# A macaron decoder layer in split float32: the first feature pair by plain products, no splits on GpSimd, and 20 weights' lower parts made ahead

## The chip, the cores and the metric

The kernel runs on one core of a Trainium2 chip. The metric is the device time of one execution in microseconds; a profiled execution gives a span (first to last instruction) and a trace. In the trace PE is the matrix engine (TensorE) and PEld its weight loads, DVE is VectorE, ACT is ScalarE, POOL is GpSimd, SP is the engine whose queue issues the kernel's DMAs.

## The reference

One layer on x of 512 tokens by 1024, all in float32:

```python
x = x + 0.5 * rms_norm(swiglu_1(rms_norm(x)))
x = x + rms_norm(hybrid_mixer(rms_norm(x)))
x = x + 0.5 * rms_norm(swiglu_2(rms_norm(x)))

def swiglu(h, w_gate, w_up, w_down):          # 1024 -> 2816 -> 1024
    return (silu(h @ w_gate) * (h @ w_up)) @ w_down
```

The mixer projects h with w_in (1024 x 2840) to the queries, keys and values of two head groups: 4 differential-attention heads, and 8 heads of sparse attention with a compressed branch (31 windows of keys and values through a small MLP, cmp_k_w1 and cmp_v_w1, 2048 x 256 each), a selected branch and a window branch. Their outputs go together through w_out.

## The kernel before, in words

**Split operands.** A float32 operand is split into a high part (a copy rounded to the matrix engine's fp32r) and a lower part (the rest), and each product is made as three: high x high, high x low, low x high. The high part is a cast on ACT (or DVE), the lower part a subtraction. `split` makes both; with `sbuf=True`, which is for sources in SBUF, the lower part may run on DVE or on POOL.

**Feed-forward.** Gate and up weights are handled in 11 pairs c of two 128-feature tiles. For a pair, the 2x2 block product (two halves of the 1024 inputs, two feature tiles, two halves of the tokens) is made with seven products in place of eight, a Winograd form of Strassen's method. It needs sums of weight blocks (`quad`, L501), sums of token blocks (`combos`, L466) and sums of the results (`tail`, L620). One product is 24 matmuls of 256 columns for gate and up together (`product`, L592). `SEQ` lists products in order; the first 12 entries weave pair 0 and pair 1. `prenorm` normalises and transposes the tokens in four blocks t; blocks 0 and 1 give the operands of products 1 and 2, and all others need blocks 2 and 3 too. The raw weights of even pairs stand in four "raw" buffers, those of odd pairs in "M" (pair 1 in "A"). The hidden tiles of the first three pairs are kept in DRAM for a while. Then `down_mm` multiplies 22 pieces of w_down (L675).

**Pieces.** `piece` loads 512 KB of a weight into a raw buffer and splits it into the ring (12 buffers, six pieces). w_down, w_in, cmp_*_w1 and w_out all come this way: pieces wp0 to 21 of the first feed-forward, 22 to 29 of w_in for keys, values and gates, 30 to 37 of the compression, 38 to 53 of w_in for the queries and the differential heads, 54 to 61 of w_out, then the second feed-forward.

**Order.** Nothing is issued in program order. `Graph.order` is a list scheduler: each operation has a cost per engine that may do it, a level (longest way to the end) plus a bias from the table `BIAS`, keyed by engine and kind of operation, and the tiles that it needs from pools of limited room (`ROOM`, `CAPS`). An operation marked `port` isn't put on DVE while one is on POOL, and the other way round, in the planner's own clock. What comes out is a fixed order for each engine's queue.

Of the kernel before, what the change touches and what calls it, by code (L numbers as in the profile page):

```python
# [40 lines left out]
WARM = (10, 0, 4)  # L41
# [18 lines left out]
    "ACT:xat>xa": 293.6, "ACT:xat>xa@ACT": 202.7, "ACT:xat>xa@DVE": 2.6, "ACT:xct>xc": 130.8, "ACT:xct>xc@ACT": 3.5,  # L60
    "ACT:xct>xc@DVE": -75.7, "ACT:xi>n_ss": 151.7, "ACT:xj>n_ss": -17, "ACT:xm>n_ss": 71.9, "ACT:xrk>Xk": 27.7,
    "ACT:xrk>Xk@ACT": 215.9, "ACT:xrk>Xk@DVE": 88.2, "ACT:xrv>Xv": 21.1, "ACT:xrv>Xv@DVE": 185.7, "ACT:z>o_ss": -397,
    "DVE:acc>oN": -22.3, "DVE:cd_t>kc": -2.6, "DVE:ck>kcT": 33, "DVE:cmask>cmb": -15, "DVE:cmask>gates": -21.9,
    "DVE:cmk>uk": -47.8, "DVE:cmv>uv": -143.2, "DVE:cv>vc": -114.3, "DVE:d>d_p": 5.9, "DVE:d_acc>o": -23.6,
    "DVE:d_r>d_p": 57.3, "DVE:d_t>d_th": -89.6, "DVE:dkt>dk": -5, "DVE:dl>d_r": 15.8, "DVE:dl>do_r": -95.2,
    "DVE:do_rr>o": 29.9, "DVE:do_t>oTd": -159.1, "DVE:fa>fh": -99.8, "DVE:fa>fhs": -11.9, "DVE:fb>fp_": -0.2,
    "DVE:fc>fp_": -0.1, "DVE:fc__sg>fh": -132.7, "DVE:fh>fhl@DVE": 14, "DVE:fh>fhl@POOL": 311.6, "DVE:fhr>fhl": 105.8,
# [10 lines left out]
    "DVE:rawff2q>fqv": -3, "DVE:rawff2q>fqw": 168, "DVE:wrv>wv": 105, "DVE:xaf0>xat": -287, "DVE:xaf1>xat": -136.2,
    "DVE:xag>xat": -23.4, "DVE:xat>xa": -88.7, "DVE:xat>xa@DVE": -123.4, "DVE:xat>xa@POOL": -416.3,
    "DVE:xat>xat": 117.5, "DVE:xcf0>xct": -36.7, "DVE:xcg>xct": 73.7, "DVE:xct>xc@DVE": -82.9, "DVE:xct>xct": -126.9,  # L80
    "DVE:xi>n_xn": 708.4, "DVE:xj>n_xn": -7.5, "DVE:xm>n_xn": 164.6, "DVE:xrk>Xk": 54.2, "DVE:xrk>Xk@DVE": -2.7,
    "DVE:xrk>Xk@POOL": -3.8, "DVE:xrv>Xv": -333.6, "DVE:xrv>Xv@POOL": 55.6, "DVE:z>o_yg": -29.8, "PE:cd>kc": 86.1,
    "PE:d_th>d_acc": 10, "PE:dkd>dk": 5.9, "PE:fqw>fa": 40.2, "PE:fqw>fb": 1946, "PE:fqw>fc": 144.3,
    "PE:gh>g_": 714.9, "PE:k__dup>kT": 107.9, "PE:n_p>n_th": 513.5, "PE:n_th>acc": 1025.2, "PE:n_xn>n_t": 678.6,
    "PE:n_xn>xa": 5.3, "PE:n_xn>xb": -7, "PE:n_xn>xc": 3.3, "PE:nc_h>acc": -114.8, "PE:nc_pc>nc_h": -56.2,
    "PE:o>oTd": 45.6, "PE:qTd>d_p": 32.9, "PE:qTn>n_p": -100.2, "PE:qTn>nc": -153.5, "PE:qdd>qTd": -46.3,
    "PE:qdn>qTn": 30.3, "PE:uk>hTk": 48.3, "PE:uv>hTv": 162.9, "PE:warm>warm": -220.7, "PE:wk>ck": 142.1,
    "PE:wp>cd": 2, "PE:wp>dkd": 3.2, "PE:wp>fc__": 5.5, "PE:wp>fy": 24.4, "PE:wp>pv": 4.5, "PE:wp>qdd": -27.8,
    "PE:wp>qdn": 241.5, "PE:wp>uk": 119.8, "PE:wp>uv": -58.6, "PE:wp>z": 7.7, "PE:wv>cv": -146.5, "POOL:Xk>Xk": -91.6,
    "POOL:Xv>Xv": -59.2, "POOL:do_r>do_rr": -5.4, "POOL:do_ss>do_r": -23.4, "POOL:n_ss>n_r": 32,  # L90
    "SP:cmask>cmask": 21.4, "SP:dmask>dmask": -101.9, "SP:fhd>fhr": -72.1, "SP:g_ff1_norm_post>g_ff1_norm_post": 29.3,
    "SP:g_ff2_norm_post>g_ff2_norm_post": -22.6, "SP:g_ff2_norm_pre>g_ff2_norm_pre": -6.7,
    "SP:g_mix_norm_post>g_mix_norm_post": 14, "SP:g_mix_norm_pre>g_mix_norm_pre": 215.9, "SP:gr>gr": 233.5,
    "SP:gsub>gsub": -81.4, "SP:pev>pev": 67.7, "SP:raw>raw": 272.8, "SP:rawff2q>rawff2q": 516.3,
    "SP:trig>trig": -45.2, "SP:wrk>wrk": 5.2, "SP:wrv>wrv": -22.2, "SP:x>xm": -63.6, "SP:x>xo": -51, "SP:xi>xi": 92.4,
    "SP:xj>x": 4.2, "SP:xj>xj": 60.7, "SP:xm>x": -19.8, "SP:xm>xm": -31, "SP:xo>xo": 30,
# [3 lines left out]
    "s_yg": 66, "s_h": 14, "s_v": 36, "s_p": 5, "s_t": 22, "s_o": 16, "s_oT": 15, "b_t": 22, "b_x": 20, "b_gu": 6, "s_ch": 8, "s_f": 10, "s_q": 8,  # L100
# [173 lines left out]
def layer(ctx: ExitStack, tc: tile.TileContext, io, out):  # L274
# [36 lines left out]
    def f32(ap):  # L311
        return ap.bitcast(F32)
# [17 lines left out]
    def piece(src, a, b, pool="ring"):  # L330
        i = len(wp)
        n = a * b
        raw, w = f"raw{i}", f"wp{i}"
        new(raw, "raw", [P, 1024])
        pdma.append(load(raw, lambda: T[raw][:, :n].rearrange("p (a b) -> p a b", a=a), src, chain="dma"))
        if pool == "ring":
            parts[i] = [f"wp{i}h", f"wp{i}l"]
            for k in parts[i]:
                new(k, pool, [P, 1024], F32R)
            hi, lo = (lambda k=k: T[k][:, :n] for k in parts[i])  # L340
        else:
# [24 lines left out]
    def split(src, hi, lo, n, r, kh, kl, chain=None, sbuf=False, after=()):  # L366
# [4 lines left out]
        def low():  # L371
            (V if o.done == "DVE" else nc.gpsimd).tensor_sub(lo(), src(), f32(hi()))  # L372
# [74 lines left out]
    def new_combos(name):  # L447
        for m in range(1, 8):
            new(f"{name}{m}", "A", [P, 2, 4, 256], F32R)

    def combos(xT, t, banks):

        u, fl = t % 2, (lambda k: (lambda: T[k].rearrange("p (k q) -> p k q", k=4)))
        cs = slice(u * P, (u + 1) * P)

# [909 lines left out]
```

## Time and profile before

| | |
|---|---|
| median of 3 runs | 1043.58 us (1043.29 to 1046.88) |
| profiled execution | 1042.48 us, span 1040.7 us |
| mean granted clock of the span | 0.990 |
| busy: PE, PEld, DVE, ACT, POOL | 97%, 88%, 75%, 53%, 10% |
| HBM read, written | 104.00 MB, 9.44 MB |

Busy time of PE is modelled from the starts of pipelined matmuls, so a PE that is busy all the time need not be at its peak. Idle time counts only on an engine that others wait for.

### The profile page before, as it was taken

The numbers are of one execution on the slowest core, as the hardware profiler recorded it, in microseconds if no ns is written. First come the engines' busy times: TensorE is split into PE (matmuls) and PEld (weight loads), VectorE is DVE, ScalarE is ACT, GpSimd is POOL, SyncE is SP. The second block draws the span as 40 slices with busy tenths as digits, with TensorE's granted clock in tenths as the row PEclk, the third lists the DMA queues.
The fourth block names the chain that finished last, engine by engine and source line by source line (L and its number), as shares of the span: only waits on it lengthen the run. The fifth ranks groups of instructions, "written<-read, shape, count | busy, mean of one in ns | idle before, by whom it ended". The sixth has DMA issues, their size and how long they took to land.

```text
span 1040.7 us, 17111 instructions
## 1 busy us (share of the span) xinstructions
PE 1005.4 (97%) x6540; PEld 913.2 (88%) x6540; DVE 783.5 (75%) x1528; ACT 548.5 (53%) x1128; POOL 104.3 (10%) x107
## 2 busy tenths in 40 slices
PE   7999999999999989899999999999999999999997
PEld 6999999999888869787888888889999999988886
DVE  6999998987332477977888799799999988743324
ACT  7554555556222254676877787485555555632302
POOL 2100000001000040131100153221000000000001
PEclk9999999999999999999999999999999999999999
DMA  7145433217432342611010236114434231473202
GB/s 243 59 145 149 147 109 123 70 53 250 175 102 81 88 143 82 223 43 60 23 40 22 60 107 238 41 42 162 139 125 146 73 108 41 143 262 101 81 21 81
DMA packets 78723, 114.53 MB, mean 110 GB/s; under 512 B 9905, under 2 KB 60337, under 8 KB 78642
## 3 DMA queue, kind: packets, MB, share of 16 engines
q1 hardware_dynamic: 78642, 113.45, 32.8%
q8 instruction: 51, 0.84, 0.3%
q14 instruction: 30, 0.25, 0.1%
HBM read 104.00 MB, written 9.44 MB: 109 GB/s over the span
## 4 chain that ended last, share of the span: by engine, by line
PE 79%; DVE 14%; issue 2%; ACT 2%; DMA 1%; POOL 1%; SPq 0%; DVEq 0%; POOLq 0%; ACTq 0%
PE ff2y L675 12%; PE ff1y L675 11%; PE ff1b L592 7%; PE ff2b L592 6%; PE ff1a L592 5%; PE ff1c L592 5%; PE ff2c L592 4%; PE ff2a L592 4%; PE z L1221 3%; PE n_t L1117 2%; PE n L1007 1%; PE acc L363 1%; PE n L1008 1%; PE acc L364 1%; DVE ff2p L620 1%
## 5 line engine op out<-in xcount | busy, mean ns | idle before, releaser
L1020 ACT ACTIVATE n_p<-n_p,n_nm 128x128 f32<-128x128 f32 (+3 forms) x64 | 35.3, 553 | 11.9 <-DVE n_nm L1018 11.5
L372 DVE TENSOR_TENSOR n_th<-n_t,n_th 128x512 fp32r<-128x512 f32 x40 | 26.0, 685 | 11.0 <-ACT n_th L369 11.0
L1018 DVE CUSTOM_DVE_ANT_0 n_p<-n,dmb 128x128 f32<-128x128 f32 (+3 forms) x64 | 28.3, 485 | 3.4 <-PE n L1008 1.6
L404 POOL TENSOR_SCALAR o_ms<-o_ss 128x1 f32<-128x1 f32 x12 | 4.5, 372 | 240.1 <-ACT junk L412 240.1
L369 ACT CAST n_th<-n_t 128x512 fp32r<-128x512 f32 x40 | 21.5, 592 | 12.9 <-PE n_t L1117 12.9
L435 PE MATMUL n_t<-ident,n_xn 128*128 128x128 f32 x96 | 15.9, 313 | 9.7 <-DVE n_xn L428 9.7
L620 DVE TENSOR_TENSOR ff1p<-ff1p,ff1b 128x512 f32<-128x512 f32 x33 | 22.5, 685 | 2.0 <-PE ff1b L592 1.9
L435 PEld LDWEIGHTS n_t<-ident,n_xn 128*128 128x128 f32 x96 | 13.0, 161 | 12.1 <-DVE n_xn L428 9.7
L620 DVE TENSOR_TENSOR ff2p<-ff2p,ff2b 128x512 f32<-128x512 f32 x33 | 22.6, 685 | 1.1 <-PE ff2b L592 1.0
L609 ACT ACTIVATE ff2p<-ff2p 128x256 f32<-128x256 f32 x33 | 13.7, 417 | 17.7 <-DVE ff2p L620 17.5
L609 ACT ACTIVATE ff1p<-ff1p 128x256 f32<-128x256 f32 x33 | 13.7, 417 | 16.0 <-DVE ff1p L620 15.7
L412 ACT ACTIVATE junk<-ff2y 128x512 bf16<-128x512 f32 x8 | 4.8, 597 | 32.3 <-PE ff2y L675 32.3
L372 POOL TENSOR_TENSOR wp1l<-raw,wp1h 128x1024 fp32r<-128x1024 f32 x1 | 2.4, 2410 | 190.2 <-PE ff1b L592 190.2
L542 DVE TENSOR_TENSOR o_yg<-ff2y,g_ff_norm_post 128x512 f32<-128x512 f32 x8 | 5.5, 689 | 21.2 <-ACT junk L412 21.2
L1020 ACT ACTIVATE d_p<-d_p,d_nm 128x128 f32<-128x128 f32 (+3 forms) x32 | 17.9, 561 | 6.7 <-DVE d_nm L1018 6.7
L372 POOL TENSOR_TENSOR wp63l<-raw,wp63h 128x1024 fp32r<-128x1024 f32 x1 | 2.4, 2405 | 188.6 <-PE ff2b L592 188.6
L1007 PE MATMUL n<-kT,qTn 128*128 128x128 f32 (+3 forms) x64 | 20.8, 338 | 0.1
L1117 PEld LDWEIGHTS n_t<-ident,n_p 128*128 128x128 f32 x160 | 18.7, 140 | 2.5
L1117 PE MATMUL n_t<-ident,n_p 128*128 128x128 f32 x160 | 20.7, 272 | 0.0
L1008 PE MATMUL n<-kT,qTn 128*128 128x128 f32 (+3 forms) x64 | 19.7, 321 | 0.0
L1018 DVE CUSTOM_DVE_ANT_0 d_p<-d,dmb 128x128 f32<-128x128 f32 (+3 forms) x32 | 15.0, 486 | 2.2 <-PE d L1008 2.1
L363 PE MATMUL acc<-n_th,v 128*64 128x512 f32 x40 | 16.7, 417 | 0.0
(1776 smaller groups left out, 3521.3 us busy)
## 6 DMA issues: line engine op xcount, KB each, us to landing
raw<-ff_w_down SPq DMA_DIRECT2D x44, 512.0 KB, 3.7
rawff1q<-ff_w_gate SPq DMA_DIRECT2D x22, 512.0 KB, 6.3
rawff1q<-ff_w_up SPq DMA_DIRECT2D x22, 512.0 KB, 5.3
rawff2q<-ff_w_gate SPq DMA_DIRECT2D x22, 512.0 KB, 5.5
rawff2q<-ff_w_up SPq DMA_DIRECT2D x22, 512.0 KB, 5.9
raw<-w_in SPq DMA_DIRECT2D x20, 512.0 KB, 4.3
raw<-w_out SPq DMA_DIRECT2D x8, 512.0 KB, 3.6
xj<-x SPq DMA_DIRECT2D x4, 512.0 KB, 8.4
```

Source lines behind the costliest of these rows:

```text
L372: (V if o.done == "DVE" else nc.gpsimd).tensor_sub(lo(), src(), f32(hi()))
L435: nc.tensor.transpose(T[b][:, k * P:(k + 1) * P], T[xn][:, k * P:(k + 1) * P], ident)
L592: nc.tensor.matmul(o, T[w][:, s, k * P:(k + 1) * P], T[xm][:, r, k, :], start=m in (1, 6, 5) and e + k + s + r == 0, stop=m in (2, 4, 3) a ...
L609: op("ACT", act(256), lambda: A.activation(T[sg][:, :256], T[sg][:, :256], AF.Silu), w=[sg])
L620: op("DVE", dve(512), lambda: fn(T[out], T[x], T[y]), r=[k for k in (x, y) if k != out], w=[out])
L675: nc.tensor.matmul(T[f"{f}y{t}{j}"], T[a[s]][:, sl], wp[i](r)[:, j, :], start=c == DOWN[0] and s + r == 0, stop=c == DOWN[-1] and s == 1)
L1007: nc.tensor.matmul(T[b][:, :L], qt[:, 0, h, :], k()[:, :L], start=True, stop=False)
L1008: nc.tensor.matmul(T[b][:, :L], qt[:, 1, h, :], k()[:, :L], start=False, stop=True)
L1018: op("DVE", dve(L), lambda: V.tensor_tensor_reduce(T[p][:, :L], T[b][:, :L], T["dmb"][:, S - L:], -1.0, 3e38, ALU.add, ALU.min, T[nm][:, 0 ...
L1020: op("ACT", act(L, 0.22), lambda: A.activation(T[p][:, :L], T[p][:, :L], AF.Exp, bias=T[nm][:, 0:1], scale=-1.0, accum_out=T[l][:, col:col ...
L1117: nc.tensor.transpose(T[bt][:, h * P:(h + 1) * P], T[p[h]][:, kb * P:(kb + 1) * P], ident)
L1221: nc.tensor.matmul(T[y[j]], T[f"oT{t}{'nd'[k < 4]}{s}"][:, k % 4, :], wp[wo[k]](r)[:, j, :], start=k == 4 and s + r == 0, stop=k == 3 and ...
```

## The change

- **Pair 0 by plain products.** `SEQ` no longer has pair 0. Eight plain block products for it (`plain`) come first in both feed-forwards: four with token blocks 0 and 1, four with blocks 2 and 3. They need no weight sums and no result sums, but one more token operand (number 8) and four PSUM banks. Pair 1's raw weights go to "M".
- **`combos`** now splits both halves of blocks 2 and 3 as well, and makes the four sums in place.
- **`split`** makes lower parts on DVE alone; the scaling of the attention rows in `nsa_branch` is no longer offered to POOL.
- **`ahead`**: for the four cmp_v_w1 pieces and 16 w_in pieces (columns 1536, 512, 0 and 1024 on), once the last product of feed-forward 1 is issued, the weight is loaded, cast on ACT, subtracted on DVE, and the lower part is stored in DRAM. The later `piece` loads the weight as before, makes the high part, and loads the lower part.
- **Three cmp_k_w1 pieces** (`KEPT`) stand in "A" rather than in the ring.
- **12 transposes** more on PE (`WARM`), six behind the transposes of token block 0, six behind those of block 1.
- **`BIAS`** is new in nearly every entry.

```diff
-WARM = (10, 0, 4)
+WARM = (10, 0, 4, 6, 6)
+KEPT = 3
...
+    def ahead(src, a, b):
+
+        i, n = len(low), a * b
+        k, d = new(f"pre{i}", ("A", "a_pre"), [P, 2, 1024], F32R), dram.tile([P, 1024], F32, name=f"low{i}")
+        raw, hi = (lambda: f32(T[k])[:, 0, :n]), (lambda: T[k][:, 1, :n])
+        load((k, 0), lambda: raw().rearrange("p (a b) -> p a b", a=a), src, chain="pre", after=[ends["ff1"]])
+        op("ACT", act(n, 0.04), lambda: A.copy(hi(), raw()), r=[(k, 0)], w=[(k, 1)])
+        op("DVE", dve(n), lambda: V.tensor_sub(T[k][:, 0, :n], raw(), f32(hi())), r=[(k, 1)], w=[(k, 0)], port=True)
+        op("SP", 1.46, lambda: nc.sync.dma_start(d[:, :n], raw()), r=[(k, 0)], w=[f"low{i}"])
+        low[i] = d
+        return i
+
+    def piece(src, a, b, pool="ring", lower=None):
...
+        if lower is None:
+            split(lambda: T[raw][:, :n], hi, lo, n, [raw], parts[i][:1], parts[i][1:], sbuf=True)
+        else:
+            def high():
+                (A.copy if h.done == "ACT" else V.tensor_copy)(hi(), T[raw][:, :n])
+
+            h = op(("ACT", "DVE"), (act(n, 0.04), 0.07 + 0.00052 * n), high, r=[raw], w=parts[i][:1], port=True)
+            op("SP", 1.46, lambda: nc.sync.dma_start(f32(lo()), low[lower][:, :n]), r=[f"low{lower}"], w=parts[i][1:], chain="dma")
...
-            o = op(("DVE", "POOL"), (dve(n), pool(n)), low, r=r + kh, w=kl, port=True)
+            o = op("DVE", dve(n), low, r=r + kh, w=kl, port=True)
...
+        for j in range(2):
+            k = new(f(t // 2, j), ("S", "s_f"), [P, 512])
+            parts(((1, 2), (8, 4))[t // 2][j], fl(banks[j]), banks[j], False)
+            op("ACT", act(512), lambda k=k, j=j: A.copy(T[k], T[banks[j]]), r=[banks[j]], w=[k])
         if t < 2:
...
+            return
+        f11, f12, f21, f22 = (f(i, j) for i in range(2) for j in range(2))
+        for m, dst, a, b, fn in ((5, f22, f21, f22, V.tensor_sub), (7, f21, f11, f21, V.tensor_sub), (6, f11, f22, f11, V.tensor_sub),
+                                 (3, f12, f12, f11, V.tensor_add)):
...
+            if c == 0:
+                src, r = blk(m // 2, m % 2), raw[m // 2]
+            else:
...
-    SEQ = [(1, 0), (1, 1), (2, 0), (2, 1), (5, 0), (6, 0), (5, 1), (7, 0), (6, 1), (4, 0), (3, 0), (7, 1)]
+    SEQ = [(1, 1), (5, 1), (6, 1), (2, 1), (7, 1)]
...
+        def plain(i, n):
+
+            x = bk("abcd"[2 * i + n], 0)
+            for j in range(2):
+                multiply(x, 0, 2 * j + n, f"{xT}{((1, 2), (8, 4))[i][j]}", j == 0, j == 1)
+            gated(0, x, n, i, True)
...
+        if t < 2:
+            warm(WARM[3 + t], after=g.writers[f"n1{t}_t1"])
...
+    low_c = {"k": (None,) * 4, "v": [ahead(*cmp_rows("v", j)) for j in range(4)]}
+    low_i = {c: [ahead(*in_rows(c, 512, j)) for j in range(4)] for c in (1536, 512, 0, 1024)}
...
-            o.append(op(("DVE", "ACT", "POOL"), (0.13 + 0.00052 * L, act(L, 0.14), 0.15 + 0.00167 * L), sc, r=[cf], w=[p[h]], port=True))
+            o.append(op(("DVE", "ACT"), (0.13 + 0.00052 * L, act(L, 0.14)), sc, r=[cf], w=[p[h]], port=True))
...
+        hidden(n, [piece(*cmp_rows(n, j), pool="A" if n == "k" and j < KEPT else "ring", lower=low_c[n][j]) for j in range(4)])
...
+    w = in_pieces(1536, 512, low_i[1536])
```

## Rows read from the trace of the kernel before

**Rows 1.** The page: busy us, share of the span, instructions of each engine.

```profile
PE 1005.4 (97%) x6540; PEld 913.2 (88%) x6540; DVE 783.5 (75%) x1528; ACT 548.5 (53%) x1128; POOL 104.3 (10%) x107
```

**Rows 2.** Stretches: us, busy of PE, PEld, DVE, ACT, POOL, clock, DMA share, GB/s.

```profile
14.50:60.00 45.50, 40.47 (x295) 39.15 (x294) 42.50 (x69) 27.72 (x52) 8.17 (x7) 0.96 0.40 136
60.00:98.50 38.50, 36.12 (x302) 35.94 (x300) 37.06 (x65) 20.90 (x40) 0.00 (x0) 1.00 0.38 103
...
253.00:362.00 109.00, 109.00 (x483) 90.23 (x482) 38.11 (x46) 29.18 (x40) 1.68 (x3) 1.00 0.39 128
362.00:420.00 58.00, 53.48 (x301) 46.70 (x300) 44.52 (x77) 31.45 (x75) 13.27 (x19) 0.97 0.30 101
418.00:432.00 14.00, 9.98 (x77) 9.12 (x76) 13.51 (x24) 7.75 (x14) 0.00 (x0) 1.00 0.72 242
440.00:480.00 40.00, 38.21 (x240) 32.41 (x239) 30.73 (x103) 26.54 (x76) 10.49 (x6) 0.96 0.23 73
...
618.00:688.00 70.00, 66.93 (x352) 56.67 (x351) 59.39 (x129) 45.07 (x122) 24.39 (x30) 0.98 0.38 139
688.00:762.00 74.00, 71.21 (x590) 70.63 (x591) 73.35 (x123) 44.13 (x84) 8.44 (x7) 1.00 0.39 129
...
253.00:260.00 7.00, 7.00 (x33) 5.77 (x32) 4.66 (x8) 2.96 (x5) 0.91 (x1) 1.00 0.91 321
```

**Rows 3.** The same view, three of the five stretches with a granted clock of 0.50.

```profile
54.60:57.80 3.20, 3.20 (x17) 3.20 (x16) 3.20 (x7) 2.47 (x5) 0.00 (x0) 0.50 1.09 379
...
378.90:382.10 3.20, 3.20 (x10) 2.55 (x9) 3.00 (x6) 2.47 (x4) 1.09 (x3) 0.50 0.35 93
...
624.70:627.90 3.20, 2.83 (x9) 2.41 (x10) 3.06 (x9) 1.45 (x3) 0.16 (x1) 0.50 0.23 93
```

**Rows 4.** Waits of PE: us in total, times, longest us.

```profile
PE n_t L435 <- DVE n_xn L428: 9.7, 5, 4.5
...
PE qTn L841 <- DVE n_nm L1018: 1.7, 1, 1.7
```

**Rows 5.** Timeline of DVE and POOL: start us, us, instruction.

```profile
356.23 1.22 DVE L372 TENSOR_TENSOR wp22l<-raw,wp22h 128x1024 fp32r<-128x1024 f32 x1 [3.42 <-PE ff1y L675]
...
368.49 0.75 DVE L428 SCALAR_TENSOR_TENSOR n_xn<-xj,n_r,g_mix_norm_pre 128x512 f32<-128x512 f32 x1
...
374.98 2.79 POOL L372 TENSOR_TENSOR wp25l<-raw,wp25h 128x1024 fp32r<-128x1024 f32 x1
375.48 2.83 DVE L428 SCALAR_TENSOR_TENSOR n_xn<-xj,n_r,g_mix_norm_pre 128x512 f32<-128x512 f32 x1
...
463.46 2.41 POOL L372 TENSOR_TENSOR wp46l<-raw,wp46h 128x1024 fp32r<-128x1024 f32 x1
463.59 3.37 DVE L372 TENSOR_TENSOR wp45l<-raw,wp45h 128x1024 fp32r<-128x1024 f32 x1
...
618.86 6.15 DVE L1197 SCALAR_TENSOR_TENSOR o<-o,do_rr,gsub 128x128 f32<-128x128 f32 x4
620.12 2.40 POOL L372 TENSOR_TENSOR wp59l<-raw,wp59h 128x1024 fp32r<-128x1024 f32 x1 [0.30 <-ACT wp59h L369]
```

**Rows 6.** Timeline of PE in the first start.

```profile
15.76 2.72 PE L592 MATMUL ff1a<-xa,ff1q00w 128*128 128x256 f32 x11 [0.64 <-DVE xa L372]
...
30.07 1.60 PE L592 MATMUL ff1a<-xa,ff1q10w 128*128 128x256 f32 x12
31.51 1.60 PE L592 MATMUL ff1a<-xa,ff1q11w 128*128 128x256 f32 x12
...
54.12 2.40 PE L592 MATMUL ff1c<-xa,ff1q00w 128*128 128x256 f32 x11 [1.31 <-POOL xa L372]
```

**Rows 7.** Timeline of DVE: two splits of 512 elements in a row.

```profile
26.36 0.68 DVE L518 TENSOR_TENSOR ff1q01w<-rawff1q,ff1q01w 128x512 fp32r<-128x512 f32 x1
26.96 0.68 DVE L518 TENSOR_TENSOR ff1q10w<-rawff1q,ff1q10w 128x512 fp32r<-128x512 f32 x1
```

**Rows 8.** Timeline of SP's queue: issue of the down weights.

```profile
264.72 65.95 SPq L319 DMA_DIRECT2D raw<-ff_w_down  x12
```

More of the change, by code (lines that the diff above doesn't have):

```diff
@@ L63 @@
[L63 to L67, printed above, removed]
@@ L78 @@
[L78 to L82, printed above, removed]
@@ new lines @@
+    "DVE:xrv>Xv@DVE": 124.3, "DVE:xrv>Xv@POOL": -18.4, "DVE:z>o_yg": 4.8, "PE:cd>kc": 28.9, "PE:d_p>o": 12.8,
+    "PE:d_th>d_acc": -4, "PE:dkd>dk": -85.6, "PE:fqw>fa": 0.5, "PE:fqw>fc": 2644, "PE:gh>g_": 1289.3,
+    "PE:k__dup>kT": -35.8, "PE:n_p>n_th": 274.9, "PE:n_th>acc": 865.9, "PE:n_xn>n_t": 23.1, "PE:n_xn>xb": -5,
+    "PE:n_xn>xc": -1.5, "PE:nc_h>acc": -32, "PE:nc_pc>nc_h": 4.7, "PE:o>oTd": 3.4, "PE:qTd>d_p": 30.9,
+    "PE:qTn>n_p": 1.4, "PE:qTn>nc": -71.1, "PE:qdd>qTd": 25.8, "PE:qdn>qTn": -14.4, "PE:uk>hTk": -9.9,
@@ L447, in new_combos @@
     def new_combos(name):
-        for m in range(1, 8):
+        for m in range(1, 9):
             new(f"{name}{m}", "A", [P, 2, 4, 256], F32R)
@@ new lines, in combos @@
+        if t < 2:
+            return
+        f11, f12, f21, f22 = (f(i, j) for i in range(2) for j in range(2))
+        for m, dst, a, b, fn in ((5, f22, f21, f22, V.tensor_sub), (7, f21, f11, f21, V.tensor_sub), (6, f11, f22, f11, V.tensor_sub),
+                                 (3, f12, f12, f11, V.tensor_add)):
+            op("DVE", dve(512), lambda dst=dst, a=a, b=b, fn=fn: fn(T[dst], T[a], T[b]), r=[k for k in (a, b) if k != dst], w=[dst],
+               port=True)
+            parts(m, fl(dst), dst, True)
@@ L483, in quad @@
     def quad(f, c, e):
         w, tag = ("gate", "up")[e], f"{f}q{c}{e}"
-        wide = c == 1
-        raw = [(f"raw{tag}", j) for j in range(2)] if wide else [f"raw{tag}{j}" for j in range(2)]
-        if wide:
-            new(raw[0][0], "A", [P, 2, 1024])
-        rt = lambda j: T[raw[j][0]][:, j] if wide else T[raw[j]]
+        raw = [f"raw{tag}{j}" for j in range(2)]
         for j in range(2):
-            if not wide:
-                new(raw[j], "M" if c % 2 else "raw", [P, 1024])
+            new(raw[j], "M" if c % 2 else "raw", [P, 1024])
@@ L579, in ffn, with multiply, mm @@
         for c in range(NP):
-            for x in "abc":
+            for x in "abc" if c else "abcd":
                 bank(bk(x, c), "b_gu")
+        def multiply(x, c, w, xm, start, stop):
+            for e in range(2):
+                k = f"{f}q{c}{e}w{w}"
+                def mm(e=e, k=k):
+                    o = T[x][:, e * 256:(e + 1) * 256]
+                    for i in range(4):
+                        for s, r in ((0, 0), (0, 1), (1, 0)):
+                            nc.tensor.matmul(o, T[k][:, s, i * P:(i + 1) * P], T[xm][:, r, i, :],
+                                             start=start and e + i + s + r == 0, stop=stop and i == 3 and s == 1, skip_group_check=True)
+                op("PE", pe(256, 12), mm, r=[(k, 0), (k, 1)] + [(xm, u, s) for u in range(2) for s in range(2)], w=[x], chain="F")
@@ L648, in ffn @@
             spill(c)
-        end = g.last["F"]
+        end = ends[f] = g.last["F"]
         for c in range(SPILL):
@@ L709, in layer, with warm @@
     bank("warm", "b_g")
-    def warm(n):
+    def warm(n, after=()):
         def f():
@@ L716, in warm @@
         if n:
-            op("PE", 0.2135 * n, f, w=["warm"], chain="W")
+            op("PE", 0.2135 * n, f, w=["warm"], chain="W", after=after)
     for j in range(2):
```

189 lines of the change are left out of this document (84 added, 105 removed), and 4 rows, old and new, of the table BIAS.

## Prediction

> **What bounds the kernel now.** I read the page first, then TensorE's (PE's) waits, the busy times by stage, and the instruction timelines around each gap. PE is busy for 97% of the span, VectorE (DVE) for 75% and GpSimd (POOL) for 10% [rows 1]. In the long middle of each feed-forward stage PE does nothing but products; 12 matmuls start 1.44 us after the 12 before them, so one product of one feature pair (24) takes 2.88 us [rows 6]. There, and in the down stage (PE 109.00 of 109.00 us [rows 2]), nothing but fewer matmuls could save time. So what the change can win lies in PE's gaps, and the stage rows show all but the head and the tail of the kernel's: the start of feed-forward 1, 45.50 less 40.47 = 5.0 us, then 2.4; the entry to the mixer 4.5; the compression weights 4.0; the first attention 1.8; the output projection 3.1; the start of feed-forward 2 2.8 [rows 2]. Together 23.6 us.
>
> Five of these gaps cost twice. After each stands a stretch with a granted clock of 0.50, that is 1.2 GHz instead of 2.4, the five alike; the first, the third and the last stand in [rows 3]. PE is nearly fully busy in them, so each stretch of about 3.4 us costs some 1.7 us (3.2 us at half speed is 1.6; the stage rows' 0.04 of 45.50 and 0.03 of 58.00 give 1.8 and 1.7 [rows 2]). The five cost 8.5 us.
>
> Who made PE wait? The named releaser is mostly DVE [rows 4]. Behind DVE stands POOL. At the mixer's entry the DVE scaling n_xn lasts 2.83 us and ends half a microsecond after POOL's split of wp25l (374.98 plus 2.79); an ordinary instruction of this form lasts 0.75 [rows 5]. In the first attention the DVE split of wp45l lasts 3.37 us and ends after POOL's split of wp46l (463.46 plus 2.41); alone, wp22l takes 1.22 [rows 5]. In the output projection four small DVE scalings of o take 6.15 us while POOL splits wp59l [rows 5]. And one gap in the first start is put down to POOL itself, which was splitting xa [rows 6]. So a split on POOL does not run beside DVE: it holds up a DVE instruction that PE is waiting for.
>
> **The change, part by part.**
>
> *Plain products for pair 0.* Eight products in place of seven, in each feed-forward: 2.88 us more PE work twice, +5.8 us, certain, as both stages are PE-bound. In exchange DVE loses, per feed-forward, 6 weight splits, 8 block sums and 5 tail additions of pair 0: 19 instructions that follow one another at 0.60 us [rows 7], 11.4 us. It gains work in the token combinations: for the last two token blocks 12 splits instead of the 10 that DVE and POOL shared. If POOL did none of those ten, DVE gains 1.2 us, if all, 7.2. More important is the order: the first eight products (23.0 us) now need no combination at all. In that cover DVE must make 8 weight splits (4.8 us), 8 sums and 12 splits of tokens (12.0 us) and four scalings (some 3.0): 19.8 us. It fits, so pair 1 should find its operands ready, and from then on DVE's load per pair is the steady one that leaves PE without a gap today. Gains: 5.0 plus a clock dip of 1.7 in the first start, 2.4 plus 1.7 around 98 us, and at the second start 2.0 of the 2.8 (bounds 0 and 2.8; I stay below the upper end, since the first splits after the transposes are unchanged).
>
> *Twelve warm-up transposes* sit behind the transposes of the first two token blocks, where PE is idle anyway, so they cost nothing as long as that idle time is there; if x came earlier, six of them would be in the way. After the idle stretch the first 11 matmuls last 2.72 us where 12 later last 1.60 [rows 6]; I read that as the lower level, though the granted clock does not show it. If the warm-up keeps the clock up, 1.2 us are saved, else 0 (2.72 less 11/12 of 1.60 is 1.2). I take 0.6, the middle, as no row is nearer to either.
>
> *No splits on POOL.* At the mixer's entry the two splits on POOL (wp24l and wp25l) hold DVE through the whole 4.5 us. DVE must now make them itself, 2 x 1.22 = 2.4 us; at worst they stand in the same gap, and 2.1 is won. But DVE is busy for 44.52 of 58.00 us there [rows 2], so they can lie earlier. I take 3.5 (bounds 2.1 and 4.5), plus the dip, 1.7: 5.2. First attention: 1.8 plus 1.7 = 3.5. Output projection: 3.1 less the 0.8 that I leave for the transposes at its end, plus 1.7: 4.0. DVE takes on POOL's output-weight splits there, up to eight at 1.22 us, in a stage where it is busy for 59.39 of 70.00 us, part of that held time.
>
> *Twenty lower parts made early.* Each is one load, one ScalarE cast, one DVE subtraction of 1.22 us and one store, in the first down stage; later a second load takes the subtraction's place. DVE's 24.4 us land where it is busy for 38.11 of 109.00 us and ScalarE for 29.18 [rows 2], so both are covered by the down products. The cover holds while SP's queue keeps the down weights coming: their 12 loads wait for free buffers, not for the DMA engines (65.95 us for 12, one per 5.5 us [rows 8]). The extra traffic is 40 transfers of 0.52 MB, 21 MB, beside 128 GB/s x 109 us = 14.0 MB: 35 MB. The best stretch carried 321 GB/s at a share of 0.91 [rows 2], 353 at full share; that is 99 us of 109. It fits, narrowly. At the compression weights (418 to 432) DVE loses six subtractions (7.3 of its 13.51 us), which speaks for winning all 4.0; but the 3.4 MB moved there grow by eight lower parts (4.2) and shrink by three kept weights (1.6) to 6.0 MB, 17.0 us at 353 GB/s, 3 us more than the stage lasts, and a dip of 1.7 on top. Bounds -4.0 and +4.7; I take 0. In the later mixer these second loads have time.
>
> *The table of priorities* is new throughout, so every queue's order changes. The trace cannot price that. It lies between no new gap and gaps like those seen: 1.7 plus a dip of 1.7 up to 4.5 plus 1.7, mean 4.8 [rows 3, 4]. I count one, +4.8.
>
> Sum: -6.7 - 0.6 - 4.1 - 2.0 - 5.2 - 3.5 - 4.0 + 0 + 5.8 + 4.8 = -15.5. The profiled execution took 1042.5 us (span 1040.7), 1.1 below the median; 1042.5 - 15.5 = **1027**.
>
> On POOL a rule speaks against the change. The Trainium skill, Perfetto Trace Analysis, section Optimizing Scalar/DVE Operations, says that work may be moved off a saturated DVE, even to GpSimd, though it warns that the two share a read port. Taken by its first half, DVE would be the loser here, and the sum would be the first rival's 1040; the held instructions above agree with the warning instead.
>
> **The rivals.**
>
> *DVE becomes the bound in the mixer.* The three gains that rest on POOL (5.2 + 3.5 + 4.0 = 12.7) don't come because DVE now carries those splits itself. For it: DVE at 59 of 70 us before the second feed-forward. Against it: those busy times contain the held time. 1027 + 12.7 = 1040.
>
> *Half the start's gain.* ScalarE's casts or the arrival of x hold the first products, and half of 6.7 + 0.6 + 4.1 is lost: 1033.
>
> *The new order brings gaps of its own.* Three more of 4.8: 1041. For it: the new priorities; against it: nothing in the trace, either way.
>
> *Slower: the DMA engines become the bound of the first down stage.* Loads and stores together may carry less than 321 GB/s. The lowest ratio in my rows is 93 GB/s at a share of 0.35, 266 [rows 3]; 35 MB then need 132 us, 22.6 more than the stage has: 1050. It decides once down weights come later than the ring's six pieces of cover, about 6 x 5.5 = 33 us. Against it: only the down weights are urgent; the lower parts may run over into the mixer.
>
> **How the numbers follow.** Forecast case 0.57, half start 0.12, DVE bound 0.10, own gaps 0.10, DMA bound 0.11. The forecast's own range takes the bounds: down by 0.6 + 1.0 + 4.0 + 0.8 + 4.8 to 1016, up by 0.6 + 1.4 + 4.7 + 2.0 + one more gap of 4.8 to 1041. The whole range is 1015 to 1044; it leaves out the DMA case and the outer end of the forecast's. 0.5% of 1043.6, about what a measurement here can tell from no change, is 5.2 us, so "faster" ends at 1038.4. Faster: 0.57 + 0.12, and half of the DVE case, 0.74. Same: the other half and the own gaps, 0.15. Slower: 0.11.
>
> **What would show it.** Right: no gap of PE and no 0.50 stretch between 45 and 110 us; the first products end some 9 us earlier than now; no POOL split anywhere, and no xj, n_xn or o instruction of DVE over 1.5 times its normal length; DVE up by some 24 us in the first down stage with PE still at 100%. Wrong: PE waiting in the first down stage for a weight or a DMA; new 0.50 stretches in the mixer; PE waiting for a second load of a lower part around 420 to 435; DVE at its limit before the second feed-forward.

## The result and the profile after

The changed kernel takes 1013.99 us (median of 4 runs, 1013.61 to 1015.08) against 1043.61 for the kernel before (4 runs): a ratio of 0.9711, 95% interval 0.969 to 0.9732. It is 29.6 us faster where 16.6 were forecast (1043.6 less 1027), and 1 us below the range. The direction was right and the size was not.

The page's busy line and TensorE's waits after the change, all of them (engine, what waited, for what: us in total, times, longest):

```profile
PE 1000.6 (99%) x6600; PEld 910.4 (90%) x6600; DVE 778.8 (77%) x1539; ACT 563.5 (56%) x1136; POOL 34.0 (3%) x68
PE warm L742 <- POOL ident masks.py:199: 1.3, 1, 1.3
PE n_t L458 <- DVE n_xn L451: 1.2, 2, 0.7
PE ff1a L606 <- DVE xa L395: 1.0, 2, 0.7
PE ff1a L606 <- ACT xa L392: 0.6, 1, 0.6
PE ff1c L606 <- DVE xa L395: 0.6, 1, 0.6
PE ff2c L606 <- DVE xc L395: 0.3, 1, 0.3
PE qn L376 <- ACT wp39h L365: 0.2, 1, 0.2
```

Read against [rows 1, 4]: the waits of several us are gone, and nothing took their place. DVE is busy about as long as before although POOL's share fell from 10% to 3%. The stages (columns as in [rows 2]: stretch, length, busy of PE, PEld, DVE, ACT, POOL, granted clock, DMA share, GB/s):

```profile
13.80:58.00 44.20, 42.60 (x349) 41.97 (x350) 44.15 (x74) 32.07 (x61) 1.38 (x3) 1.00 0.44 151
58.00:96.00 38.00, 38.00 (x319) 38.00 (x318) 35.90 (x63) 19.03 (x35) 0.00 (x0) 1.00 0.46 132
242.70:350.00 107.30, 107.30 (x476) 88.87 (x475) 60.78 (x66) 48.52 (x57) 0.00 (x0) 1.00 0.92 327
350.00:406.00 56.00, 55.94 (x327) 49.26 (x326) 45.81 (x95) 33.97 (x80) 9.23 (x18) 1.00 0.48 161
406.00:420.00 14.00, 13.76 (x100) 11.96 (x99) 8.67 (x27) 8.88 (x22) 0.00 (x0) 1.00 1.03 406
430.00:470.00 40.00, 40.00 (x244) 33.18 (x243) 32.55 (x122) 28.57 (x84) 0.00 (x0) 1.00 0.37 132
590.00:660.00 70.00, 69.90 (x391) 59.87 (x390) 64.78 (x154) 50.28 (x138) 14.75 (x24) 1.00 0.38 130
660.00:740.00 80.00, 79.66 (x665) 79.42 (x664) 76.12 (x129) 47.25 (x90) 2.33 (x4) 1.00 0.42 138
```

Line by line beside [rows 2]: the first start still loses 1.6 us, the rest of the list under 0.4 us each, and the clock column is 1.00 in every stage: with the gaps the five 0.50 stretches of [rows 3] went. In the first down stage DVE does 22.7 us more, about what the twenty subtractions take, and the DMA engines are busy for 92% of 107 us while PE does not wait once.

Where along the kernel the time went is read from the first matmul of five groups (view of the tiles, after; of each line the number ahead of "to"):

```profile
L606 PE MATMUL ff1a<-xa,ff1q00w x24: 274/283/387, 13.8 to 20.1; 128*128 128x256 f32 x24
L703 PE MATMUL ff1y<-wp0h,ff1hh x8: 389/389/397, 242.7 to 247.1; 128*128 128x512 f32 x8
L376 PE MATMUL pa<-wp22h,xb x8: 389/389/478, 361.3 to 383.5; 128*128 128x512 f32 x8
L606 PE MATMUL ff2a<-xc,ff2q00w x24: 278/283/363, 659.5 to 663.8; 128*128 128x256 f32 x24
L703 PE MATMUL ff2y<-wp62h,ff2hh x8: 389/389/397, 886.2 to 890.5; 128*128 128x512 f32 x8
```

The same lines of before begin at 14.5, 252.6, 378.8, 688.3 and 914.5 us. So:

| stretch | predicted | measured |
| --- | --- | --- |
| to the first down product (first start, 98 us, plain products +2.9) | -8.5 | -9.9 |
| to the first mixer product (entry) | -5.2 | -7.6 |
| to the first product of feed-forward 2 (compression 0, attention -3.5, output -4.0) | -7.5 | -11.3 |
| to the second down stage (second start -2.0, plain products +2.9) | +0.9 | +0.5 |
| to the end | 0 | -0.2 |
| the new order's own gap, wherever it falls | +4.8 | none found |
| sum | -15.5 | -28.5 |

Of the 13.0 us that the forecast missed, 4.8 are the order's term, 3.8 lie in the mixer's middle, 2.4 at its entry, 1.4 in the first start and 0.6 behind the middle. The border between entry and middle is not the same place in both kernels: before, the first mixer product follows the last down product and 16 transposes; after, nine matmuls of the down stage (364.80 to 367.1) and eight of these transposes come behind it. That is the new order at work: ready products stand where the gap was.

### The profile page after: what moved, and what is told of

The parts are those of the page before. It is cut to its first block, busy times and chain, and to the rows that moved or that the text cites. A ratio compares the mean times of both kernels' runs of the same rounds, so it can differ in the third digit from the quotient of the medians.

```text
span 1012.2 us, 17253 instructions
## 1 busy us (share of the span) xinstructions
PE 1000.6 (99%) x6600; PEld 910.4 (90%) x6600; DVE 778.8 (77%) x1539; ACT 563.5 (56%) x1136; POOL 34.0 (3%) x68
## 5 line engine op out<-in xcount | busy, mean ns | idle before, releaser
L341 DVE TENSOR_TENSOR pre<-pre 128x1024 fp32r<-128x1024 f32 x20 | 24.2, 1222 | 25.3 <-ACT pre L340 25.1
L340 ACT CAST pre<-pre 128x1024 fp32r<-128x1024 f32 x20 | 21.0, 1052 | 30.0 <-DMA pre<-w_in 23.2
L1057 DVE CUSTOM_DVE_ANT_0 n_p<-n,dmb 128x128 f32<-128x128 f32 (+3 forms) x64 | 28.5, 485 | 4.5 <-PE n L1047 4.1
L392 ACT CAST n_th<-n_t 128x512 fp32r<-128x512 f32 x40 | 21.6, 593 | 14.9 <-PE n_t L1154 14.9
L645 DVE TENSOR_TENSOR ff2p<-ff2p,ff2b 128x512 f32<-128x512 f32 x30 | 20.4, 679 | 1.5 <-PE ff2b L606 1.5
L645 DVE TENSOR_TENSOR ff1p<-ff1p,ff1b 128x512 f32<-128x512 f32 x30 | 20.4, 679 | 1.1 <-PE ff1b L606 1.0
L633 ACT ACTIVATE ff2p<-ff2p 128x256 f32<-128x256 f32 x30 | 12.5, 417 | 14.3 <-DVE ff2p L645 13.5
L633 ACT ACTIVATE ff1p<-ff1p 128x256 f32<-128x256 f32 x30 | 12.5, 416 | 13.3 <-DVE ff1p L645 12.5
L387 PE MATMUL acc<-n_th,v 128*128 128x512 f32 x40 | 15.7, 392 | 0.0
L645 DVE TENSOR_TENSOR ff2p<-ff2c,ff2p 128x512 f32<-128x512 f32 x20 | 13.7, 687 | 2.5 <-PE ff2c L606 2.2
```

What stands on the lines that cost most here:

```text
L340: op("ACT", act(n, 0.04), lambda: A.copy(hi(), raw()), r=[(k, 0)], w=[(k, 1)])
L341: op("DVE", dve(n), lambda: V.tensor_sub(T[k][:, 0, :n], raw(), f32(hi())), r=[(k, 1)], w=[(k, 0)], port=True)
L392: (A.copy if h.done == "ACT" else V.tensor_copy)(hi(), src())
L633: op("ACT", act(256), lambda: A.activation(T[sg][:, :256], T[sg][:, :256], AF.Silu), w=[sg])
L645: op("DVE", dve(512), lambda: fn(T[out], T[x], T[y]), r=[k for k in (x, y) if k != out], w=[out])
L1057: op("DVE", dve(L), lambda: V.tensor_tensor_reduce(T[p][:, :L], T[b][:, :L], T["dmb"][:, S - L:], -1.0, 3e38, ALU.add, ALU.min, T[nm][:, 0 ...
```

## Experiments

The theory under test: a split on POOL holds DVE, the plain pair gives DVE time, and the order is a small, unknown loss. The rival: POOL's work is replaced by work on DVE, and what closed the gaps is the early lower parts or the order. One rival has no run: the kernel before with a table made for it anew. How much of the 29.6 us a better order alone would have given it stays open.

| run | median, us | ratio to before, 95% interval |
| --- | --- | --- |
| e1: before, POOL's splits on DVE | 1038.21 | 0.9943 (0.9922 to 0.9963) |
| e2: after, ten splits on POOL | 1022.28 | 0.9788 (0.9759 to 0.9817) |
| e3: after, no early lower parts | 1028.91 | 0.9849 (0.9811 to 0.9886) |
| e12: after, 4 of 20 made at use | 1017.49 | 0.9734 (0.969 to 0.9779) |
| e13: after, the other 16 made at use | 1024.13 | 0.9796 (0.9755 to 0.9837) |
| e4: after, old table | 1067.38 | 1.0223 (1.0193 to 1.0253) |
| e17: e4 with one order edit | 1044.09 | 0.9986 (0.9962 to 1.0009) |
| e10: after without the plain pair | 1038.03 | 0.9941 (0.9917 to 0.9965) |
| e14: e10 with the old table | 1054.64 | 1.0091 (1.0062 to 1.012) |
| e11: before with the plain pair | 1071.98 | 1.0267 (1.0238 to 1.0297) |
| e8: after, no new warm-up | 1014.23 | 0.9715 (0.9686 to 0.9743) |
| e9: after, lower parts stored twice | 1026.54 | 0.9832 (0.9803 to 0.986) |

Before ran at 1043.4 to 1044.0 in these sessions, so medians of different sessions compare to about half a us.

### What POOL's splits cost: e1 and e2

Both keep the planned order and change only which engine gets the instruction. e1, in the kernel before (its small scalings of `nsa` go to DVE too):

```diff
-            (V if o.done == "DVE" else nc.gpsimd).tensor_sub(lo(), src(), f32(hi()))
+            V.tensor_sub(lo(), src(), f32(hi()))
```

> The kernel before in its own planned order, but the 33 operations that stood on GpSimd (20 weight splits, 9 token splits, 3 attention splits, and the small scalings) are issued by VectorE at the same places in the program. Theory A, a split on GpSimd holds VectorE: although VectorE now does some 35 us more, the gaps at the mixer's entry, in the first attention, in the output projection and around 98 us shrink with their dips, 8 to 16 us in all, so 1028 to 1035 us. Rival B, GpSimd did relieve VectorE and the gain of the change came from the plain pair, the early lower parts and the new order: no gain, 1043 us or more.

Measured: 1038.21, 5.8 us less than before in the same session (1044.03). The direction is theory A's, the size below its range. The mixer's entry in e1, DVE's timeline (start, us, instruction):

```profile
373.60 0.75 DVE L428 SCALAR_TENSOR_TENSOR n_xn<-xj,n_r,g_mix_norm_pre 128x512 f32<-128x512 f32 x1
374.26 0.69 DVE L372 TENSOR_TENSOR xb<-n_t,xb 128x512 fp32r<-128x512 f32 x1
374.86 1.22 DVE L372 TENSOR_TENSOR wp24l<-raw,wp24h 128x1024 fp32r<-128x1024 f32 x1
```

n_xn is back at 0.75 from the 2.83 of [rows 5], and wp24l costs DVE 1.22. From windows of 4 us (idle time of PE plus what a clock below 1.00 lost in them; windows that lose under 0.3 us are left out), e1 wins 5.9 us at the entry, 3.4 in the first attention, 2.8 in the output projection. It gives back 1.8 at the compression weights (the old gap, now with a dip) and 2.9 in the second feed-forward's start; the first start stays as it was. So 12.1 of the prediction's 12.7 us for POOL are there, but DVE's additional work costs some of them elsewhere, and taking the splits off POOL does not help the first start.

e2 is the reverse, in the changed kernel:

```diff
+ON_POOL = {"wp24l", "wp25l", *(f"wp{i}l" for i in range(56, 64))}
...
-            V.tensor_sub(lo(), src(), f32(hi()))
+            (nc.gpsimd if kl[0] in ON_POOL else V).tensor_sub(lo(), src(), f32(hi()))
```

> The changed kernel in its own order, but ten of its splits are issued by GpSimd at the same places: two of the mixer's first weights (wp24l, wp25l) and the eight output weights (wp56l to wp63l). Theory A: VectorE is held for some 2.4 us by each, the gaps at the mixer's entry and in the output projection come back with a 0.50 stretch behind them, plus 5 to 12 us, 1019 to 1026 us. Rival B, GpSimd relieves VectorE: 1014 us within 1, or less.

Measured: 1022.28, 8.3 us more than after; theory A. The entry lost 1.6 us without the 0.50 stretch that was expected there, the output projection 5.6 with one. In the output projection of e2, DVE's and POOL's timelines and the PE instruction that waited:

```profile
589.65 2.41 POOL L396 TENSOR_TENSOR wp56l<-raw,wp56h 128x1024 fp32r<-128x1024 f32 x1 [213.28 <-PE pv L378]
589.88 2.19 DVE L1182 SCALAR_TENSOR_TENSOR d_r<-d_r,nlam,dl 128x1 f32<-128x1 f32 x1
...
593.74 2.41 POOL L396 TENSOR_TENSOR wp57l<-raw,wp57h 128x1024 fp32r<-128x1024 f32 x1
594.21 0.13 DVE L1181 RECIPROCAL d_r<-dl 128x1 f32<-128x1 f32 x1
...
596.09 5.43 DVE L1235 SCALAR_TENSOR_TENSOR o<-o,do_rr,gsub 128x128 f32<-128x128 f32 x4
596.12 2.38 POOL L396 TENSOR_TENSOR wp58l<-raw,wp58h 128x1024 fp32r<-128x1024 f32 x1
602.32 1.11 PE L1242 MATMUL do_t<-ident,o 128*128 128x128 f32 x4 [3.82 <-DVE d_nm L1058]
```

An instruction on one column (d_r, two operands in SBUF) ends with the split beside it after 2.19 us, where the changed kernel has 0.22; one o takes 0.35 us undisturbed, four take 5.43 here. The reciprocal, which reads one operand, keeps its 0.13 us beside wp57l. PE waits 3.82 us and a dip of 1.7 follows. Hence a split on POOL can hold DVE for its 2.4 us when DVE's next instruction reads two operands from SBUF, against 1.22 us for making the split on DVE. The warning of the Trainium skill's Perfetto Trace Analysis, section Optimizing Scalar/DVE Operations, that work moved between these two might not help because they share a read port, agrees with it.

### What the early lower parts bring: e3, e12, e13

All three keep the order of the changed kernel, which was planned without these later subtractions; so what they lose holds for that order, and a plan made for them might lose less. The early load, cast, subtraction and store of the chosen weights are left out, and the second load becomes a subtraction behind the cast; e3 does it for all twenty, e12 for the four of the v compression, e13 for the sixteen projection weights (the cut shows e12 and e13; e3 has the subtraction without the condition):

```diff
             def high():
                 (A.copy if h.done == "ACT" else V.tensor_copy)(hi(), T[raw][:, :n])
+                if lower in AT_USE:
+                    V.tensor_sub(lo(), T[raw][:, :n], f32(hi()))
```

> The changed kernel in its own order without the 20 lower parts made early: their loads, casts, subtractions and stores in the first down stage are gone, and each second load is replaced by a VectorE subtraction behind the cast. Theory A, the early lower parts closed the gap at the compression weights (4.0 us before) because VectorE had too much to do in the mixer: that gap and others come back, plus 4 to 10 us, 1018 to 1024 us. Rival B, they bring nothing, since VectorE has room in the mixer and only GpSimd held it: 1014 us within 2.

> The changed kernel in its own order; only the lower parts of the four weights of the v compression are made at use by VectorE instead of early. Theory A, the 15 us of the run without any early lower part are spread by stage, and these four are those of the compression stage, where the prediction counted 0: a gap of 2 us with a dip of 1.7 there and nothing elsewhere, 1016 to 1020 us. Rival B, the compression stage is held by what VectorE does in the queue for the later weights, so these four alone cost nothing: 1014 us within 1.

> The changed kernel in its own order; the sixteen lower parts of the four projection weights (query, key, value of the second attention and the first query) are made at use, the four of the compression stay early. Theory A: no gap at the compression weights, but those around 452 to 464 and 500 to 516 us stay, 1022 to 1026 us. Rival B: all gaps of the run without any early lower part, 1027 to 1029 us.

Measured: 14.9, 3.5 and 10.1 us more than after. By time theory A each time; e3 went beyond its range, and the two parts nearly add up to the whole. By place it was not all as expected: the dip in e12 did not come, and e13 loses 2.2 us at 408 to 424 us, where no gap was expected. In e3 the windows lose 5.6 us at the compression weights, 4.2 in the first attention and 4.4 between 500 and 516 us, where the kernel before has no gap, but nothing at the mixer's entry. e12 shows the mechanism, DVE's timeline and PE's wait:

```profile
403.81 1.22 DVE L369 TENSOR_TENSOR wp35l<-raw,wp35h 128x1024 fp32r<-128x1024 f32 x1
...
405.40 1.22 DVE L369 TENSOR_TENSOR wp36l<-raw,wp36h 128x1024 fp32r<-128x1024 f32 x1
406.54 1.22 DVE L399 TENSOR_TENSOR wp33l<-raw,wp33h 128x1024 fp32r<-128x1024 f32 x1
PE cmk L390 <- DVE wp33l L399: 2.0, 1, 2.0
```

wp33l is a weight of the k compression that PE needs now; the two subtractions ahead of it on DVE's queue belong to v. In the changed kernel DVE starts wp33l at 402.42, 4.1 us earlier; 2.4 of these are the two subtractions. So the early parts do not shorten PE's work; they take 1.22 us each off a queue that PE waits for.

### What the order is worth: e4, e17, and the plain pair under either table: e10, e14, e11

e4 is the changed kernel with the whole table `BIAS` of the kernel before, which has no entries for the new operations; two lines of it are shown:

```diff
...
-    "PE:d_th>d_acc": -4, "PE:dkd>dk": -85.6, "PE:fqw>fa": 0.5, "PE:fqw>fc": 2644, "PE:gh>g_": 1289.3,
...
+    "PE:d_th>d_acc": 10, "PE:dkd>dk": 5.9, "PE:fqw>fa": 40.2, "PE:fqw>fb": 1946, "PE:fqw>fc": 144.3,
...
```

> The changed kernel, planned with the priority table of the kernel before (entries for operations that are new are missing). Theory A, the structure of the change carries the gain and any order would do: 1014 to 1020 us. Rival B, the order that the new table gives is a condition of the gain: gaps of 2 to 4 us with dips of 1.7 in several places, 1025 to 1045 us.

Measured: 1067.38, 53 us more than after and 23 more than before; rival B, far beyond its range. The largest gap is at the start of feed-forward 2; PE's timeline in e4, with the last two links of the chain that PE waited for:

```profile
703.96 1.60 PE L605 MATMUL ff2b<-xc,ff2q01w 128*128 128x256 f32 x12
705.40 2.91 PE L1257 MATMUL z<-wp,oT3d 128*128 128x512 f32 x12
708.16 1.03 PE L457 MATMUL n_t<-ident,n_xn 128*128 128x128 f32 x8
714.32 0.85 POOL L427 TENSOR_TENSOR n_r<-n_ms,mhalf 128x1 f32<-128x1 f32 x1
721.46 1.41 DVE L450 SCALAR_TENSOR_TENSOR n_xn<-xm,n_r,g_ff_norm_pre 128x512 f32<-128x512 f32 x2
722.26 1.97 PE L457 MATMUL n_t<-ident,n_xn 128*128 128x128 f32 x8 [13.07 <-DVE n_xn L450]
```

From the last output projection z to the last transposes n_t runs a chain over ScalarE, POOL and DVE. The four plain products that need only the first two token blocks (eight groups of 12 matmuls, 11.5 us) had been used up before z, and PE stood for 13.07 us. Some 6.3 us of this are DVE's order: n_r is ready at 715.17, and n_xn stands on DVE behind sums and splits until 721.46. In the windows of 4 us from 716 to 728 its granted clock is 0.50. The changed kernel has them behind z:

```profile
655.57 2.89 PE L1258 MATMUL z<-wp,oT3d 128*128 128x512 f32 x12
...
659.52 1.67 PE L606 MATMUL ff2a<-xc,ff2q00w 128*128 128x256 f32 x12
...
669.67 1.60 PE L606 MATMUL ff2b<-xc,ff2q01w 128*128 128x256 f32 x12
671.11 1.47 PE L458 MATMUL n_t<-ident,n_xn 128*128 128x128 f32 x12
```

e17 makes that one thing so in e4, by a dependence of the first plain products on the last z (`g.last["P"]` at that point):

```diff
-                op("PE", pe(256, 12), mm, r=..., w=[x], chain="F")
+                op("PE", pe(256, 12), mm, r=..., w=[x], chain="F",
+                   after=[g.last["P"]] if f == "ff2" and c == 0 else ())
```

> The changed kernel with the old table, as in the run of 1067 us, with one edit: the first eight plain products of feed-forward 2 may not be planned ahead of the last output projection. Theory A, in that run these products were used up before the last projection, so that nothing covered the chain from there to the last four transposes (a gap of 13.1 us and some 8 us of 0.50 clock); the edit gives 12 to 20 us back: 1047 to 1055 us. Rival B, VectorE's order sets that gap, and it stays: 1063 us or more.

Measured: 1044.09, 23.3 us back, above theory A's range; in e17 these four products (the "eight" of the expectation are their groups of 12) stand at 686.75 to 698.3 and the n_t behind them wait for nothing. One dependence was worth 23 us; 21.4 of them lie in the windows from 680 to 740 us. It makes the planner order every queue anew, and in e17 n_xn follows its n_r at once (694.06 us), so the cover and DVE's order are not separated. The rest of e4's loss stays spread over smaller gaps; one of them, of 2.6 us and with a 0.50 stretch behind it, lies at 28 to 40 us in the first start.

e10 leaves the plain pair out of the changed kernel (`combos`, `quad` and `ffn` as before, the rest as after); e14 is e10 with the old table; e11 is the kernel before with the plain pair alone, old table:

```diff
-        for m, c in [(m, 0) for m in (0, 2, 1, 3)] + SEQ:
+        for m, c in SEQ:
```

> The changed kernel without the plain pair: feature pair 0 again by seven products with the token combinations and block sums of the kernel before; no split on GpSimd, early lower parts, warm-up and the new priority table stay (entries that only the old combinations have come from the old table). Theory A, only the plain pair gives VectorE the time to make the combinations: 5.8 us of products are saved, but the gaps of the kernel before at 52 to 60 and 96 to 104 us come back with their dips in the first feed-forward, 4.4 and 4.1 us, and some 4 us at the second start: 1016 to 1024 us. Rival B, the order and the absence of GpSimd closed these gaps: 1008 us.

> As the run without the plain pair (no split on GpSimd, early lower parts, warm-up), but planned with the table of the kernel before, which was made for the seven products of pair 0 (entries of new operations come from the new table). Theory A, what the plain pair brings is hidden behind the wrong table in that run; with a fitting one the first start and the second start have the gaps of the kernel before and the mixer has none: 1043.4 less some 12 us in the mixer, 1028 to 1034 us. Rival B, the plain pair is worth more than its 5.8 us of products under any table: 1036 us or more.

> The kernel before with the plain pair and its new token combinations alone; splits on GpSimd, no early lower parts, no second warm-up, the old priority table (entries for new operations come from the new one). Theory A, the plain pair closes the gaps at 52 to 60 and 96 to 104 us whatever the rest: 5.8 us more products, 8.5 us of gaps and dips less in the first feed-forward, 1038 to 1044 us. Rival B, an old order does not fit the new operations, as the run with the old table had it: new gaps in the two starts and more in the mixer, 1050 us or more.

Measured: 1038.03, 1054.64 and 1071.98. e10 missed both of its theories, e14 and e11 went to their rivals B. Most of e11's 28.6 us is the hole of e4 again: PE waits 12.9 us for n_xn at 712 to 726 us, with 0.50 behind it. PE's largest wait in e10, and the stretch from 60 to 104 us in e10 and in e17 (columns as in [rows 2]):

```profile
PE ff1b L564 <- DVE ff1p L592: 4.8, 1, 4.8
60.00:104.00 44.00, 37.45 (x298) 37.10 (x297) 42.94 (x76) 22.41 (x44) 0.00 (x0) 0.96 0.41 115
60.00:104.00 44.00, 44.00 (x369) 44.00 (x369) 40.98 (x72) 22.90 (x41) 0.00 (x0) 1.00 0.48 136
```

With seven products the stretch from 20 to 104 us loses 9.9 us in the kernel before (windows of 4 us, idle plus clock as above), 9.7 in e1, 10.9 in e10 and 12.0 in e14: four orders, with splits on POOL and without. With the plain pair it loses 0.6 in the changed kernel but 9.6 in e17 under the old table, all of it before 60 us: from 60 to 104 us PE waits in no run with the plain pair (e4, e11 and e17 have the old table), and in every run without it. So the pair closed the gap around 98 us under all orders tried; the start before 60 us needs an order that uses its cover as well. How much of the 24 us between e10 and after is the pair and how much a table that was not made for seven products, these runs do not separate.

### The warm-up: e8

```diff
-            for _ in range(n):
+            for _ in range(n if emit else 0):
...
-            warm(WARM[3 + t], after=g.writers[f"n1{t}_t1"])
+            warm(WARM[3 + t], after=g.writers[f"n1{t}_t1"], emit=False)
```

> The changed kernel in its own order, with the twelve new warm-up transposes left out. Theory A, they keep TensorE from a slow start: the first eleven products take some 2.7 us again instead of 1.57, so 1015 us, 1 us more. Rival B, the loads set the start and the warm-up brings nothing: 1014 us within 0.3.

Measured: 1014.23 against 1013.99, rival B by the median; the single executions of either kernel range over 1.5 to 2.2 us. The first products of e8, and behind the dots the first group of products of pair 1 in e8 and then in the changed kernel:

```profile
13.99 3.44 PE L606 MATMUL ff1a<-xa,ff1q00w 128*128 128x256 f32 x12 [0.62 <-ACT xa L392]
17.23 2.76 PE L606 MATMUL ff1a<-xa,ff1q01w 128*128 128x256 f32 x12
...
42.95 1.60 PE L606 MATMUL ff1a<-xa,ff1q10w 128*128 128x256 f32 x12
41.12 1.60 PE L606 MATMUL ff1a<-xa,ff1q10w 128*128 128x256 f32 x12
```

Theory A's slow products are there, 2.76 where the changed kernel has 1.60. With the warm-up PE waits more for xa (1.6 us at ff1a against 0.6), but it stays ahead: by 1.8 us at the first group of pair 1 and by 1.4 at the end of the profiled executions (spans 1012.2 and 1013.6). So the two traces show a gain that the medians, 0.24 us apart, do not; four executions each are too few to tell.

### How near the DMA limit: e9

```diff
             nc.sync.dma_start(d[:, :n], raw())
+            nc.sync.dma_start(d2[:, :n], raw())
```

> The changed kernel with every early lower part stored twice (the second time to a DRAM tile that nothing reads): 10.5 MB more in the first down stage, some 30 us of the DMA engines at the 352 GB/s that they carried there. Theory A, the DMA engines were full there and the cover of the down weights nearly used: TensorE waits for down weights or, behind them, for the mixer's first weights, plus 5 to 30 us. Rival B, only the down weights are urgent and the rest runs over into the mixer: 1014 us within 2.

Measured: 1026.54, 12.5 us more; theory A. What waited is hardly a down weight (PE's waits for those are 0.4 us in all). ScalarE's timeline around the first mixer weights, e9, and the PE instruction that came late:

```profile
345.18 1.05 ACT L398 CAST wp23h<-raw 128x1024 fp32r<-128x1024 f32 x1 [0.64 <-DMA raw<-w_in]
356.62 1.05 ACT L398 CAST wp24h<-raw 128x1024 fp32r<-128x1024 f32 x1 [10.39 <-DMA raw<-w_in]
...
359.44 0.59 ACT L441 ACTIVATE junk<-ff1y 128x512 bf16<-128x512 f32 x1
366.40 1.97 PE L464 MATMUL n_t<-ident,n_xn 128*128 128x128 f32 x8 [8.35 <-DVE n_xn L457]
```

and the same cast in the changed kernel:

```profile
341.55 1.05 ACT L392 CAST wp24h<-raw 128x1024 fp32r<-128x1024 f32 x1 [6.18 <-DMA raw<-w_in]
```

The cast of wp24 stands ahead of the squares (junk) of the norm on ScalarE's queue. It waits for its load 6.18 us in the changed kernel already, unseen; 15.1 us later in e9, it holds the norm and PE loses 8.35 us and a clock stretch. So by estimate the change had about 6.7 us (15.1 less 8.35) left before its DMA traffic cost time.

## Why the prediction was off

- **POOL holds DVE**: right (e1, e2). Its three gains came, and DVE took over POOL's splits at 1.22 us each.
- **Plain products**: the 48 matmuls more are there (6600 less 6540, less the 12 transposes), and the cover was right in mechanism. The gap around 98 us closed with the pair under every table; the first start closed only under the new one, and the second start needs the cover as well (e17).
- **Warm-up**: 0.6 predicted; 1.8 in the traces, 0.2 in the medians (e8). The reading behind it was short: in the kernel before, the 8 transposes behind the slow 11 products took 1.91 us (1.03 later) and the 12 products behind those 1.92 (1.60), another 1.2 us. This fits 1.2 of the 1.4 us missed in the first start.
- **The step that failed is the order's term**: "I count one, +4.8". The prediction took the new table as something that could only add gaps of the size seen. The changed kernel has no gap of its own: behind the first 20 us PE's longest wait is 0.6 us. The runs show the order as a condition of the gain: the same structure under the old table is 53 us slower, one dependence gives 23 of them back, and the plain pair put into the kernel before makes it 28.6 us slower. Each of these pairs a structure with a table not made for it, so they show that the order must fit the structure, not how many of the 29.6 us are the order's own.
- **Compression weights, 0 predicted**: the second term that was mis-sized. The gap went, 4.0, the lower bound. The argument against it divided 6.0 MB by 353 GB/s, scaled from one stretch to a DMA share of 1.00; its own rows have 379 GB/s at 1.09 [rows 3]. The stage of the changed kernel moves 406 GB/s at 1.03 (406:420 above), so its transfers fit. A figure of the Trainium skill agrees with the higher rate: Perfetto Trace Analysis, section Roofline, puts the 16 DMA engines at about 435 GB/s together.
- **Early lower parts**: counted as covered and worth nothing beyond those 4.0; without them the same order loses 14.9 us (e3), with waits mostly for DVE. The rival "DVE becomes the bound in the mixer" is what happens then, at the compression weights, in the first attention and behind it. The gains at the entry and in the output projection hardly depend on the early parts (e3 loses under 0.2 us there); that of the first attention depends on the order, since e1 had it without them and e3 lost it.
- **Bounds not taken**: 1.0 was cut from the mixer's entry for work that DVE would do in the gap, and 0.8 from the output projection for the transposes at its end. Both gaps closed whole; in e1 the entry gave 5.9 us with wp24l and wp25l on DVE.
- **The slower rival**: the traffic came as forecast, 35 MB in 107 us at a share of 0.92, but the engines carried 327 GB/s, and 388 in e9, where the rival needed less than 321. Its victim was wrong as well: down weights hardly made PE wait even in e9, and the first thing that would be late is a mixer weight, some 6.7 us away (e9).

## What to carry to other kernels

When a change comes with a new order of the queues, price the order as part of the gain: ask of each gap which ready work could stand in it, and whether the change creates such work. An engine that looks free because its stage has room can still be the one that PE waits for through its queue, so moving 1.22 us pieces out of that queue paid here even at three transfers each. And a stage whose PE never waits can still be a few us from a DMA limit; find which load is latest and what stands behind it in an in-order queue.

## What the runs showed of the hardware

- A split on POOL, which reads two operands from SBUF, held the DVE instructions beside it that read two operands from SBUF as well, whatever their size (2.19 us for one column in e2; n_xn, wp45l and o in [rows 5]). A DVE instruction with one operand kept its length (the reciprocal in e2, 0.13), and so did one that reads an operand from PSUM, in e2 under wp24l:

```profile
365.67 2.38 POOL L396 TENSOR_TENSOR wp24l<-raw,wp24h 128x1024 fp32r<-128x1024 f32 x1 [3.69 <-PE ff1y L704]
366.96 0.69 DVE L396 TENSOR_TENSOR xb<-n_t,xb 128x512 fp32r<-128x512 f32 x1 [0.91 <-ACT xb L393]
```

- Loads and stores together ran at 406 GB/s for 14 us in the changed kernel, beside PE at 13.76 of 14.00.
- In e8 the second twelve products after the idle head took 2.76 us against 1.60 later, in windows whose granted clock reads 1.00: a slow start of PE is read from the length of its instructions, not from the clock column alone.
